# Moving the tiles of a two-layer hybrid block to other SBUF addresses

## The chip, the cores and the metric

The kernel runs on one NeuronCore of a Trainium2 chip. The metric is the device time of one execution in microseconds (us). The kernel before was timed three times: 1871.41, 1870.98 and 1871.26 us, a median of 1871.26 us. A profiled execution of it took 1871.55 us, and the trace's span, from the first instruction to the last, is 1869.8 us of that.

## The reference

The reference computes two layers of a hybrid block on 512 tokens of width 1024, in float32. Cut to what matters:

```python
def hybrid_layer(x, ...):
    h = rms_norm(x, g_pre_mix)
    proj = h @ w_in                                  # 1024 -> 6728 columns
    q, k, v, qi, ki, wi, xr, gr, zu, zv, gate_logits = split(proj)
    q, k, qi, ki = partial rope of each
    y_a = dsa_attention(q, k, v, qi, ki, wi)         # top 128 keys by an indexer, softmax, values
    y_b = rg_lru(causal_depthwise_conv(xr)) * gelu(gr)
    y_c = chunked_spatial_gating(gelu(zu), rms_norm(gelu(zv)), w_spatial, b_spatial)
    branch = einsum('nbsw,nwd->nbsd', stack([y_a, y_b, y_c]), w_branch)
    merged = einsum('bsnd,nbsd->bsd', sigmoid(gate_logits), branch)
    x = x + rms_norm(merged @ w_out, g_post_mix)
    f = square(relu(rms_norm(x, g_pre_ffn) @ w_ffn_up)) @ w_ffn_down
    x = x + rms_norm(f, g_post_ffn)
    ple = (p_i @ w_ple) * sigmoid(x @ w_ple_gate)
    return x + rms_norm(ple, g_post_ple)
```

## The kernel before

**Products in three passes.** Activations are held transposed: 8 tiles of 128 features by 512 tokens. Each float32 operand is split into a high part that fits the matmul's fp32r type and a low rest, and each product is made of three matmuls into one PSUM bank: high weights with high activations, low weights with high activations, high weights with low activations. That is `mm3` (lines 289 to 292), called by `gemm` once for each 128 rows of the contraction:

```python
def mm3(ps, wh, wl, xh, xl, start, stop):
    PE.matmul(ps, wh, xh, start=start, stop=False)     # L290
    PE.matmul(ps, wl, xh, start=False, stop=False)     # L291
    PE.matmul(ps, wh, xl, start=False, stop=stop)      # L292
```

The second argument is the stationary operand (128 x 128, loaded anew for each matmul, PEld in the profile) and the third is the moving operand, 512 columns wide in most calls and 256 in some. `gemm_arriving` (matmuls on L348) does the same for four outputs at a time while its input tiles are still being made. `tokens` (L585) swaps the roles: slices of the activations are stationary and the weights move.

**Weights.** 303 weight tiles of 128 x 1024 float32 come from HBM on SP's queue into a rotation of three buffers `wr`. ScalarE (ACT) casts each into `wh` (L235) and VectorE (DVE) makes the rest `wl` (L236); `wh` and `wl` have four buffers each. `getw` starts the preparation three tiles ahead.

**Activations.** `xh0` to `xl7` hold the split input of a gemm. Slots `A0` to `A7`, `B0` to `B7` (512 columns each), `K0`, `K1`, `V0`, `V1` (4 x 512 columns each) and `M0` to `M7` are used again and again: for queries and keys, for the branches' outputs, for the merged value, and for the hidden layer of the feed-forward part. `tmp` is a rotation of 11 tiles of 128 x 512 for everything short-lived. `sacc` sums squares for the norms, which GpSimd (POOL) adds up on L390.

**Order.** Every engine runs its own queue in the order in which the program issues its instructions, and waits on semaphores where a tile is read or is to be written again. The side work (index scores, top 128, attention, recurrence) is issued in pieces between the matmuls by a small planner, `tick` and `run_tasks`, with due times written in the code.

**Where a tile lies.** Three pools hold the SBUF tiles: `cp` (persistent tiles, slots and small vectors), `wp` (`wr`, `wh`, `wl`) and `tp` (`tmp`). The pools follow each other in one column of addresses, the same in all 128 partitions. Within a pool, tiles lie in the order in which they are first asked for, each padded to 32 bytes. So a small vector asked for between two large tiles shifts all that follows. A tile of 128 bytes that nothing uses, `lead`, stands ahead of `xh0`. A 512-column float32 tile takes 2048 bytes of a partition. The remainder of a tile's address after division by 2048 is called its offset from here on.

Of the kernel before, what the change touches and what calls it, by code (L numbers as in the profile page):

```python
# [8 lines left out]
F32 = mybir.dt.float32  # L9
F32R = mybir.dt.float32r  # L10
BF16 = mybir.dt.bfloat16
I32 = mybir.dt.int32
# [5 lines left out]
S = 512  # L18
D = 1024
KT = 8  # L20
# [22 lines left out]
NVEC = 76  # L43


def f32v(ap):
    return ap.bitcast(F32)
# [3 lines left out]
def hybrid_block_kernel(ctx, tc, xT, pT, pos, vec, bsp, freq, w_in, w_tok, w_lru, w_sp, w_br, w_out, w_up, w_dn, w_ple, w_gate, out, depth=DEPTH, dbg=None):  # L51
# [3 lines left out]
    cp = ctx.enter_context(tc.tile_pool(name="cp", bufs=1))  # L55
    wp = ctx.enter_context(tc.tile_pool(name="wp", bufs=1))
    tp = ctx.enter_context(tc.tile_pool(name="tp", bufs=1))
    pp = ctx.enter_context(tc.tile_pool(name="pp", bufs=1, space=PSUM))

    uid = [0]  # L60

    def nm(p):
        uid[0] += 1
        return f"{p}_{uid[0]}"

    def tmp(dt=F32):
        return tp.tile([128, S], dt, tag="tmp", name=nm("tmp"), bufs=NTMP)

    def small(n, tag="sm", bufs=8):
        return cp.tile([128, n], F32, tag=tag, name=nm(tag), bufs=bufs)  # L70

    def bank():
        return pp.tile([128, 512], F32, tag="ps", name=nm("ps"), bufs=8)

    def slot(tag, dt=F32, big=False):
        return cp.tile([128, 4, S] if big else [128, S], dt, tag=tag, name=nm(tag))
# [8 lines left out]
    NWB = 4  # L85
    LAG = 1
    TAIL = 3
    ATT = 13
    WARM = 120
    FIRST = [0, 1, 4]  # L90


    X = [cp.tile([128, S], F32, tag=f"X{k}", name=f"X{k}") for k in range(KT)]
    ident = cp.tile([128, 128], F32, tag="ident", name="ident")
    make_identity(nc, ident)
    warm = cp.tile([128, 1], F32, tag="warm", name="warm")
    V.memset(warm, 0.0)
    A.activation(warm, warm, AF.Square)
    ones2 = cp.tile([128, 2], F32, tag="ones2", name="ones2")
    V.memset(ones2, 1.0)  # L100
    mhalf = cp.tile([128, 4], F32, tag="mhalf", name="mhalf")
    V.memset(mhalf, -0.5)
    BIAS = [cp.tile([128, 128 * (t + 1)], BF16, tag=f"bias{t}", name=f"bias{t}") for t in range(4)]

    V.memset(BIAS[3], 1.0)
    wps = bank()
    for _ in range(WARM):
        PE.matmul(wps[:, 0:64], BIAS[3][:, 0:128], BIAS[3][:, 0:64], start=True, stop=True)


    tri = BIAS[0]
    G.memset(tri, 0.0)
    G.affine_select(out=tri, in_=tri, compare_op=ALU.is_ge, fill=NEG, base=0, pattern=[[-1, 128]], channel_multiplier=1)
    fq = cp.tile([128, 8], F32, tag="fq", name="fq")
    posi = cp.tile([128, 4], I32, tag="posi", name="posi")

    ropeC = cp.tile([128, S], F32, tag="ropeC", name="ropeC")
    ropeS = cp.tile([128, S], F32, tag="ropeS", name="ropeS")

# [104 lines left out]
    def prep():  # L224
        i = nprep[0]
        nprep[0] += 1
        key, src = order[i]
        raw = wp.tile([128, 1024], F32, tag="wr", name=nm("wr"), bufs=3)
        nc.sync.dma_start(raw, src)
        if key[0] == "sp":  # L230
            r3 = raw.rearrange("p (g t) -> p g t", g=8)
            G.affine_select(out=r3, in_=r3, compare_op=ALU.is_ge, fill=0.0, base=0, pattern=[[0, 8], [1, 128]], channel_multiplier=-1)
        hi = wp.tile([128, 1024], F32R, tag="wh", name=nm("wh"), bufs=NWB)
        lo = wp.tile([128, 1024], F32R, tag="wl", name=nm("wl"), bufs=NWB)
        A.copy(hi, raw)  # L235
        V.tensor_sub(lo, raw, f32v(hi))  # L236
        prepared[key] = (hi, lo)
# [15 lines left out]
    def defer(us, fn):  # L253
        later.append((clk[0] + us, uid[0], fn))
        uid[0] += 1
# [8 lines left out]
    def add_task(q, gen):  # L264
        q["wait"].append(gen)
# [17 lines left out]
    def finish(q):  # L283
        run_later(force=True)
        while q["act"] or q["wait"]:
            tick(0.3)
# [39 lines left out]

    def gemm_arriving(keys, xs, source, ranges, arrived=None, lag=LAG, tail=TAIL):


        n = len(keys)  # L330
        ws = [getw(key, 0) for key in keys[:-1]]
        pss = [bank() for _ in keys]
        last = {}
        for r in ranges:
            gen = source(r)
            for k in range(KT):
                with ordered(last):
                    next(gen)
                    todo = [(o, k) for o in range(len(ws))]
                    if len(ws) < n and k == lag:  # L340
                        ws.append(getw(keys[-1], 0))
                        todo += [(n - 1, q) for q in range(k + 1)]
                    if r is ranges[-1] and k >= KT - tail:
                        todo = [] if k < KT - 1 else [(o, q) for o in range(n) for q in range(KT - tail, KT)]
                    for i, (o, q) in enumerate(todo):
                        h3, l3 = [v.rearrange("p (k c) -> p k c", k=KT) for v in ws[o]]
                        for m in range(3):
                            PE.matmul(pss[o][:, r], (h3, l3, h3)[m][:, q], xs[q][m // 2][:, r], start=q == 0 and m == 0, stop=q == KT - 1 and m == 2)  # L348
                        if r is ranges[-1] and q == KT - 1 and o < n - 1:
                            prep()  # L350
                tick(0.65 * len(todo) * width(r) / S)
            if arrived is not None:
                arrived(r)
        while nprep[0] < nget[0] + LA:
            prep()
        return pss
# [103 lines left out]
                tick(0.1)  # L460
            return self.gens[r.start]


    cp.tile([128, 32], F32, tag="lead", name="lead")
    XS = [(slot(f"xh{k}", F32R), slot(f"xl{k}", F32R)) for k in range(KT)]

    def x_tiles(r, xs, g=None, st=None, ys=None, bc=None, gp=None, on_g=()):
# [3 lines left out]
        def updated(d):  # L471
            if ys is not None and d < KT:
                if gp is None:
                    V.tensor_mul(ys[d][:, r], ys[d][:, r], bc)
                else:
                    V.scalar_tensor_tensor(ys[d][:, r], ys[d][:, r], gp[:, d:d + 1], bc, op0=ALU.mult, op1=ALU.mult)
                (G if d in on_g else V).tensor_add(X[d][:, r], X[d][:, r], ys[d][:, r])  # L477

        updated(0)
        for d in range(KT):  # L480
            x = X[d][:, r]
            if xs is not None:
# [14 lines left out]
                    V.scalar_tensor_tensor(lo, x, g[:, d:d + 1], f32v(hi), op0=ALU.mult, op1=ALU.subtract)  # L497
            yield d

    vecs = [cp.tile([128, NVEC], F32, tag=f"vec{l}", name=f"vec{l}") for l in range(depth)]  # L500
    nc.sync.dma_start(vecs[0], vec[0])
    nc.scalar.dma_start(posi, pos)
    nc.scalar.dma_start(fq, freq)

    chunks = []
    for key, src in order[:3]:
        raw = wp.tile([128, 1024], F32, tag="wr", name=nm("wr"), bufs=3)
        hi = wp.tile([128, 1024], F32R, tag="wh", name=nm("wh"), bufs=NWB)
        lo = wp.tile([128, 1024], F32R, tag="wl", name=nm("wl"), bufs=NWB)
        prepared[key] = (hi, lo)  # L510
        chunks.append((src, raw, hi, lo))
    nprep[0] = 3
    for k in range(KT):
        if k in FIRST:
            c = slice(128 * k, 128 * (FIRST + [KT])[FIRST.index(k) + 1])
            for src, raw, hi, lo in chunks:
                nc.sync.dma_start(raw[:, c], src[:, c])
        nc.sync.dma_start(X[k], xT[k])

# [8 lines left out]
    for l in range(depth):  # L528
# [19 lines left out]
        rt = st.rt  # L548
        first = gemm_arriving([("in", l, f"xr{j}") for j in range(3)], XS, norm.source if l else lambda r: gen0, HALVES if l else (FULL,), st.row(D, R), 0, TAIL if l else 1)

        def proj(name, ahead=LA):
            ps = bank()
            gemm(ps, getw(("in", l, name), ahead), XS, KT)
            return ps
# [11 lines left out]
        def rope(ps, n=128):  # L566
            t1, u = tmp(), tmp()
            V.tensor_mul(t1[:n], ps[:n], Cr[:n])
            V.stream_shuffle(u[:n], ps[:n], mask=SHUF)
            G.tensor_mul(u[:n], u[:n], Sr[:n])  # L570
            G.tensor_add(t1[:n], t1[:n], u[:n])  # L571
            return t1
# [108 lines left out]
        def select(t, sc):  # L681
# [20 lines left out]
            G.tensor_add(gt[:, :n], gt[:, :n], eq[:, :n])  # L702
            G.tensor_scalar(BIAS[t], gt[:, :n], -NEG, NEG, op0=ALU.mult, op1=ALU.add)
            yield 1.0
# [47 lines left out]
        for j in range(4):  # L752
            mx = tmp()
# [49 lines left out]
        sp8 = small(4, "sp8", 2)  # L803
        V.tensor_scalar(sp8, h, 8.0, None, op0=ALU.mult)
        nsp8 = small(4, "nsp8", 2)
# [86 lines left out]
        def attention(j):  # L892
# [6 lines left out]
            def logits(t):  # L899
                n = 128 * (t + 1)  # L900
                pr = qk(q2, kk, (ql, ql), kk, slice(t * 128, (t + 1) * 128), max(n, 256))
                for s in range(2):
# [5 lines left out]

                    V.tensor_tensor_reduce(lt, pr[s][:, :n], BIAS[t], scale=-ATT_SCALE, scalar=3.0e38, op0=ALU.add, op1=ALU.min, accum_out=mx[:, 0:1])
                    A.activation(lt, lt, AF.Exp, scale=-1.0, bias=mx[:, 0:1], accum_out=mx[:, 1:2])  # L910
# [82 lines left out]
        for j in range(4):  # L993
            f = rope(proj(f"q{j}"))
# [8 lines left out]
            if j == 0:  # L1003
                finish(idxq)
            defer(ATT, lambda j=j: add_task(attq, attention(j)))
            gated(1, YB, ds=range(2 * j, 2 * j + 2))
# [113 lines left out]
        gp = small(8, "gp", 2)  # L1120
# [12 lines left out]
    for r in HALVES:  # L1133
        for d in norm.source(r):
            (nc.sync if d % 2 == 0 else nc.scalar).dma_start(out[d, :, r], X[d][:, r])

# [76 lines left out]
```

## Time and profile before

| | before |
|---|---|
| median of three runs | 1871.26 us (1870.98 to 1871.41) |
| the profiled execution | 1871.55 us |
| its span in the trace | 1869.8 us |
| PE busy | 1825.9 us (98%), 8798 matmuls |
| PEld busy (weight loads) | 1503.1 us (80%), 8798 loads |
| DVE, ACT, POOL busy | 1158.4, 802.4, 365.8 us (62, 43, 20%) |
| DMA | 167.77 MB, mean 90 GB/s; the weights' queue 27% of the 16 engines' span |
| TensorE clock | 0.992 of full speed on average |

PE is TensorE's matmuls, PEld its weight loads, which run beside them. Matmuls overlap in the trace: one that "takes" 391 ns is followed by the next after some 230 ns. So the pace of TensorE is read from the distance between starts, not from the mean duration.

### The profile page before, as it was taken

The page shows a single profiled execution, that of the slowest core. Times are in us where ns is not written, and L with a number is a line of the kernel's source. Part 1 is how long each engine was busy: PE and PEld are TensorE (multiplying, and loading weights), DVE is VectorE, ACT ScalarE, POOL GpSimd, SP SyncE. Part 2 cuts the span into 40 slices and gives each one's busy share as a digit, 9 for nine tenths or more (in the row PEclk, how much of TensorE's full clock was granted, in tenths as well). Part 3 has the DMA queues.
Part 4 walks back from the last instruction along what each step waited for, and adds up shares of the span by engine and source line. Part 5 has one row for each costly group of instructions (what it writes and reads, how often), then busy time and mean ns, then how long its engine had stood idle before and what let it go on. Part 6 is the DMA issues. An engine that isn't in the chain of part 4 may idle for free.

```text
span 1869.8 us, 22869 instructions
## 1 busy us (share of the span) xinstructions
PE 1825.9 (98%) x8798; PEld 1503.1 (80%) x8798; DVE 1158.4 (62%) x1939; ACT 802.4 (43%) x1292; POOL 365.8 (20%) x292
## 2 busy tenths in 40 slices
PE   8999999999999999999999999999999999999997
PEld 7678777788888888888886787887888888888886
DVE  6689976666286253533686999666563852535355
ACT  5466436564453222223444572455544432222233
POOL 3513222210240000003454141222003200000033
PEclk9999999999999999999999999999999999999998
DMA  5122222222223322332212222222222223232321
GB/s 171 62 91 84 97 91 91 68 80 79 86 84 104 100 93 99 95 109 90 91 58 95 69 90 99 94 80 69 90 79 91 91 90 102 92 100 92 111 79 57
DMA packets 49679, 167.77 MB, mean 90 GB/s; under 512 B 6049, under 2 KB 8865, under 8 KB 49569
## 3 DMA queue, kind: packets, MB, share of 16 engines
q1 hardware_dynamic: 47376, 163.64, 27.0%
q10 hardware_dynamic: 2192, 2.67, 0.5%
q8 instruction: 69, 1.13, 0.3%
q14 instruction: 42, 0.34, 0.1%
HBM read 164.19 MB, written 2.10 MB: 89 GB/s over the span
## 4 chain that ended last, share of the span: by engine, by line
PE 74%; DVE 11%; POOL 6%; issue 5%; ACT 4%; DMA 0%; SPq 0%; POOLq 0%; ACTq 0%; DVEq 0%
PE ps L290 21%; PE ps L292 20%; PE ps L291 20%; PE ps L348 4%; PE ps L585 4%; DVE tmp L689 2%; DVE wl L236 2%; DVE m L687 2%; POOL tmp L570 1%; POOL tmp L571 1%; PE ps L937 1%; PE ps L654 1%; PE ps L651 1%; POOL sacc L390 1%; POOL X L477 1%
## 5 line engine op out<-in xcount | busy, mean ns | idle before, releaser
L235 ACT CAST wh<-wr 128x1024 fp32r<-128x1024 f32 x303 | 317.0, 1049 | 468.7 <-PE ps L292 382.8
L236 DVE TENSOR_TENSOR wl<-wr,wh 128x1024 fp32r<-128x1024 f32 x303 | 386.2, 1278 | 201.8 <-ACT wh L235 201.7
L290 PE MATMUL ps<-xh,wh 128*128 128x512 f32 (+1 forms) x1296 | 506.9, 391 | 0.0
L292 PE MATMUL ps<-xl,wh 128*128 128x512 f32 (+1 forms) x1296 | 498.1, 384 | 0.0
L291 PE MATMUL ps<-xh,wl 128*128 128x512 f32 (+1 forms) x1296 | 495.7, 382 | 0.8 <-DVE wl L236 0.8
L390 POOL TENSOR_TENSOR sacc<-sacc,tmp 128x256 f32<-128x256 f32 (+1 forms) x99 | 110.3, 1115 | 902.9 <-issue 590.1
L292 PEld LDWEIGHTS ps<-xl,wh 128*128 128x128 f32 x1296 | 243.4, 188 | 50.1
L290 PEld LDWEIGHTS ps<-xh,wh 128*128 128x128 f32 x1296 | 243.7, 188 | 49.4 <-issue 4.9
L291 PEld LDWEIGHTS ps<-xh,wl 128*128 128x128 f32 x1296 | 243.7, 188 | 46.9 <-DVE wl L236 1.7
L292 PE MATMUL ps<-V,wh 128*128 128x512 f32 (+1 forms) x528 | 196.8, 373 | 0.0
L290 PE MATMUL ps<-K,wh 128*128 128x512 f32 (+1 forms) x432 | 159.9, 370 | 0.0
L291 PE MATMUL ps<-K,wl 128*128 128x512 f32 (+1 forms) x432 | 157.9, 366 | 0.0
L292 PE MATMUL ps<-B,wh 128*128 128x512 f32 x336 | 131.9, 392 | 0.0
L290 PE MATMUL ps<-A,wh 128*128 128x512 f32 x320 | 126.6, 396 | 0.0
L291 PE MATMUL ps<-A,wl 128*128 128x512 f32 x320 | 124.8, 390 | 0.0
L1072 DVE TENSOR_TENSOR M<-M,ps 128x512 f32<-128x512 f32 x48 | 33.1, 689 | 143.8 <-PE ps L292 143.8
L292 PEld LDWEIGHTS ps<-V,wh 128*128 128x128 f32 x528 | 99.3, 188 | 18.5
L1060 DVE TENSOR_TENSOR tmp<-ps,R 128x512 f32<-128x512 f32 x64 | 43.8, 689 | 111.5 <-PE ps L292 111.5
L348 PE MATMUL ps<-xl,wh 128*128 128x256 f32 (+1 forms) x264 | 88.4, 335 | 7.8 <-DVE xl L497 7.2
L291 PEld LDWEIGHTS ps<-K,wl 128*128 128x128 f32 x432 | 81.2, 188 | 14.3
L290 PEld LDWEIGHTS ps<-K,wh 128*128 128x128 f32 x432 | 81.3, 188 | 13.2
L348 PE MATMUL ps<-xh,wh 128*128 128x256 f32 (+1 forms) x264 | 87.1, 330 | 0.5 <-ACT xh L487 0.5
(239 smaller groups left out, 2745.5 us busy)
## 6 DMA issues: line engine op xcount, KB each, us to landing
wr<-in_w_in_dram SPq DMA_DIRECT2D x95, 512.0 KB, 3.3
wr<-in_w_up_dram SPq DMA_DIRECT2D x64, 512.0 KB, 3.3
wr<-in_w_dn_dram SPq DMA_DIRECT2D x64, 512.0 KB, 3.3
wr<-in_w_br_dram SPq DMA_DIRECT2D x24, 512.0 KB, 3.3
wr<-in_w_tok_dram SPq DMA_DIRECT2D x16, 512.0 KB, 3.3
wr<-in_w_out_dram SPq DMA_DIRECT2D x16, 512.0 KB, 3.3
wr<-in_w_gate_dram SPq DMA_DIRECT2D x16, 512.0 KB, 3.3
X<-in_xT_dram SPq DMA_DIRECT2D x8, 256.0 KB, 5.8
```

The costliest lines, as they stand in the source:

```text
L235: A.copy(hi, raw)
L236: V.tensor_sub(lo, raw, f32v(hi))
L290: PE.matmul(ps, wh, xh, start=start, stop=False)
L291: PE.matmul(ps, wl, xh, start=False, stop=False)
L292: PE.matmul(ps, wh, xl, start=False, stop=stop)
L348: PE.matmul(pss[o][:, r], (h3, l3, h3)[m][:, q], xs[q][m // 2][:, r], start=q == 0 and m == 0, stop=q == KT - 1 and m == 2)
L390: G.tensor_add(sacc[:, r], sacc[:, r], self.q[r.start, r.stop])
L585: PE.matmul(ps, x, w, start=k == 0 and i == 0, stop=k == KT - 1 and i == 2)
L687: V.max(m8, (sc if r == 0 else wk)[:, :n])
L689: V.match_replace(wk[:, :n], m8, (sc if r == 0 else wk)[:, :n], -3.0e38)
L1060: V.tensor_mul(t, ps, R)
L1072: V.tensor_add(F[d], F[d], ps)
```

## The change

No instruction is added, removed or moved. On every engine the order of instructions and what each waits for are the same as before, but for one name: the tile that a first ACT instruction warms up with is now one of the `sm` vectors. Only the addresses of the tiles differ:

- All small vectors (`sm`, `rt`, `wi`, `m8`, `cnt`, `sp8`, `nsp8`, `mx`, `gp`, `vec0`) are asked for first and lie at the head of `cp`. The constants and masks (`ident`, `ones2`, `mhalf`, the bias tiles, `fq`, `posi`, `vec1`) go to a new pool `ep`, behind `tmp`.
- An unused tile of 256 bytes fills `cp` up so that `X0` begins at 18432, which is 9 x 2048. What follows in `cp`, and `wr` behind it, comes in tiles of 2048, 4096 or 8192 bytes.
- Behind `wr` an unused tile of 128 bytes shifts `wh`, `wl` and `tmp`.

The offsets, address modulo 2048 bytes, before and after:

| tiles | before | after |
|---|---|---|
| `X0` to `X7` | 128 | 0 |
| `ropeC`, `ropeS`, `sacc` | 1312 | 0 |
| `xh`, `xl` | 1440 | 0 |
| `R` | 160 | 0 |
| `B0` to `B7`, `M0`, `M1`, `M4` to `M7` | 416 | 0 |
| `A0` to `A7`, `K0`, `K1`, `V0`, `V1` | 672 | 0 |
| `M2`, `M3` | 928, 1056 | 0 |
| `wr` | 1376 | 0 |
| `wh`, `wl`, `tmp` | 1376 | 128 |

A weight tile of 4096 bytes is read in slices of 128 columns, 512 bytes apart, so a stationary slice lies at 1376 plus a multiple of 512 before and at 128 plus a multiple of 512 after.

```diff
@@ pools
     tp = ctx.enter_context(tc.tile_pool(name="tp", bufs=1))
+    ep = ctx.enter_context(tc.tile_pool(name="ep", bufs=1))
@@ head of the kernel
+    LEAD = 256
+    GAP = 32
...
-    X = [cp.tile([128, S], F32, tag=f"X{k}", name=f"X{k}") for k in range(KT)]
-    ident = cp.tile([128, 128], F32, tag="ident", name="ident")
+    for n, tag, bufs in ((4, "sm", 8), (4, "rt", 4), (32, "wi", 2), (8, "m8", 4), (1, "cnt", 4), (4, "sp8", 2), (4, "nsp8", 2), (2, "mx", 8), (8, "gp", 2)):
+        small(n, tag, bufs)
+    vecs = [(ep if l else cp).tile([128, NVEC], F32, tag=f"vec{l}", name=f"vec{l}") for l in range(depth)]
+    gap = [False]
+
+    def wraw():
+        raw = wp.tile([128, 1024], F32, tag="wr", name=nm("wr"), bufs=3)
+        if not gap[0]:
+            gap[0] = True
+            wp.tile([128, GAP], F32, tag="gap", name="gap")
+        return raw
+    ident = ep.tile([128, 128], F32, tag="ident", name="ident")
...
-    BIAS = [cp.tile([128, 128 * (t + 1)], BF16, tag=f"bias{t}", name=f"bias{t}") for t in range(4)]
+    BIAS = [ep.tile([128, 128 * (t + 1)], BF16, tag=f"bias{t}", name=f"bias{t}") for t in range(4)]
...
+    cp.tile([128, LEAD // 4], F32, tag="lead", name="lead")
+    X = [cp.tile([128, S], F32, tag=f"X{k}", name=f"X{k}") for k in range(KT)]
     ropeC = cp.tile([128, S], F32, tag="ropeC", name="ropeC")
...
@@ prep, and the first three weight tiles
-        raw = wp.tile([128, 1024], F32, tag="wr", name=nm("wr"), bufs=3)
+        raw = wraw()
@@ ahead of xh0
-    cp.tile([128, 32], F32, tag="lead", name="lead")
     XS = [(slot(f"xh{k}", F32R), slot(f"xl{k}", F32R)) for k in range(KT)]
```

## Rows read from the trace of the kernel before

**Rows 1.** The page: engines' busy time, share of the span, instructions.

```profile
PE 1825.9 (98%) x8798; PEld 1503.1 (80%) x8798; DVE 1158.4 (62%) x1939; ACT 802.4 (43%) x1292; POOL 365.8 (20%) x292
```

**Rows 2.** The page: the chain that ended last, by engine.

```profile
PE 74%; DVE 11%; POOL 6%; issue 5%; ACT 4%; DMA 0%; SPq 0%; POOLq 0%; ACTq 0%; DVEq 0%
```

**Rows 3.** Timeline of PE, a feed-forward gemm: start, us, engine, line, tiles.

```profile
630.27 0.39 PE L290 MATMUL ps<-K,wh 128*128 128x512 f32 x1
...
652.24 0.40 PE L290 MATMUL ps<-K,wh 128*128 128x512 f32 x1
```

**Rows 4.** The same view, a feed-forward gemm on `A` and `B`.

```profile
700.31 0.39 PE L290 MATMUL ps<-A,wh 128*128 128x512 f32 x1
...
722.28 0.39 PE L290 MATMUL ps<-A,wh 128*128 128x512 f32 x1
```

**Rows 5.** The chain in order of time: start, us, engine, line, count.

```profile
886.24 21.97 PE ps L348 x96
```

**Rows 6.** Timeline of PE, the output projection, the same tiles as in the feed-forward gemm.

```profile
471.96 0.40 PE L290 MATMUL ps<-K,wh 128*128 128x512 f32 x1
...
494.36 0.40 PE L290 MATMUL ps<-K,wh 128*128 128x512 f32 x1
```

**Rows 7.** Timeline of PE, `tokens`: weights move, activations are stationary.

```profile
233.04 0.39 PE L585 MATMUL ps<-wh,xh 128*128 128x512 f32 x1
...
237.24 0.39 PE L585 MATMUL ps<-wh,xh 128*128 128x512 f32 x1
```

**Rows 8.** Timeline of PE, `tokens` in a stretch at the lower clock.

```profile
1003.89 0.63 PE L585 MATMUL ps<-wl,xh 128*128 128x512 f32 x1
...
1006.03 0.63 PE L585 MATMUL ps<-wh,xl 128*128 128x512 f32 x1
```

**Rows 9.** Busy time by stretch, PE alone: that stretch, with its granted clock.

```profile
1003.90:1006.40 2.50, 2.50 (x7) 0.50 0.85 252
```

**Rows 10.** Timeline of PE, spatial gating, 256 columns, weights move.

```profile
130.28 0.28 PE L290 MATMUL ps<-wh,K 128*128 128x256 f32 x1
...
130.63 0.28 PE L290 MATMUL ps<-wh,K 128*128 128x256 f32 x1
...
130.98 0.28 PE L290 MATMUL ps<-wh,K 128*128 128x256 f32 x1
...
132.91 0.28 PE L292 MATMUL ps<-wl,K 128*128 128x256 f32 x1
```

**Rows 11.** Timeline of PE, a gemm in halves, 256 columns.

```profile
1839.73 0.28 PE L290 MATMUL ps<-xh,wh 128*128 128x256 f32 x1
...
1840.91 0.28 PE L291 MATMUL ps<-xh,wl 128*128 128x256 f32 x1
```

**Rows 12.** Groups by line and shape, PE: count, busy us, mean ns, idle before.

```profile
L290 PE MATMUL ps<-xh,wh 128*128 128x512 f32 x1200 | 479.8, 400 | 0.0
...
L585 PE MATMUL ps<-wh,xh 128*128 128x512 f32 x128 | 53.2, 415 | 0.0
...
L292 PE MATMUL ps<-A,wh 128*128 128x512 f32 x64 | 25.4, 397 | 0.0
```

**Rows 13.** The same view, 256 columns.

```profile
L348 PE MATMUL ps<-xl,wh 128*128 128x256 f32 x176 | 52.4, 298 | 4.0 <-DVE xl L497 3.5
...
L292 PE MATMUL ps<-V,wh 128*128 128x256 f32 x96 | 26.8, 279 | 0.0
```

**Rows 14.** The same view, DVE, 512 columns.

```profile
L1061 DVE SCALAR_TENSOR_TENSOR tmp<-tmp 128x512 f32<-128x512 f32 x64 | 43.8, 689 | 1.6
L1060 DVE TENSOR_TENSOR tmp<-ps,R 128x512 f32<-128x512 f32 x64 | 43.8, 689 | 111.5 <-PE ps L292 111.5
...
L362 DVE TENSOR_TENSOR B<-tmp,A 128x512 fp32r<-128x512 f32 x32 | 21.9, 684 | 0.0
...
L362 DVE TENSOR_TENSOR V<-tmp,K 128x512 fp32r<-128x512 f32 x32 | 21.5, 683 | 1.4 <-ACT K L361 1.4
```

**Rows 15.** The page: DMA queues, then the weights' issues with time to landing.

```profile
q1 hardware_dynamic: 47376, 163.64, 27.0%
...
wr<-in_w_in_dram SPq DMA_DIRECT2D x95, 512.0 KB, 3.3
```

More of the change, by code (lines that the diff above doesn't have):

```diff
@@ L90, in hybrid_block_kernel @@
     FIRST = [0, 1, 4]
-    X = [cp.tile([128, S], F32, tag=f"X{k}", name=f"X{k}") for k in range(KT)]
-    ident = cp.tile([128, 128], F32, tag="ident", name="ident")
+    for n, tag, bufs in ((4, "sm", 8), (4, "rt", 4), (32, "wi", 2), (8, "m8", 4), (1, "cnt", 4), (4, "sp8", 2), (4, "nsp8", 2), (2, "mx", 8), (8, "gp", 2)):
[9 more added lines that the diff above has]
+    ident = ep.tile([128, 128], F32, tag="ident", name="ident")
     make_identity(nc, ident)
-    warm = cp.tile([128, 1], F32, tag="warm", name="warm")
+    warm = small(1)
     V.memset(warm, 0.0)
     A.activation(warm, warm, AF.Square)
-    ones2 = cp.tile([128, 2], F32, tag="ones2", name="ones2")
+    ones2 = ep.tile([128, 2], F32, tag="ones2", name="ones2")
     V.memset(ones2, 1.0)
-    mhalf = cp.tile([128, 4], F32, tag="mhalf", name="mhalf")
+    mhalf = ep.tile([128, 4], F32, tag="mhalf", name="mhalf")
     V.memset(mhalf, -0.5)
-    BIAS = [cp.tile([128, 128 * (t + 1)], BF16, tag=f"bias{t}", name=f"bias{t}") for t in range(4)]
+    BIAS = [ep.tile([128, 128 * (t + 1)], BF16, tag=f"bias{t}", name=f"bias{t}") for t in range(4)]
     V.memset(BIAS[3], 1.0)
@@ L113, in hybrid_block_kernel @@
     G.affine_select(out=tri, in_=tri, compare_op=ALU.is_ge, fill=NEG, base=0, pattern=[[-1, 128]], channel_multiplier=1)
-    fq = cp.tile([128, 8], F32, tag="fq", name="fq")
-    posi = cp.tile([128, 4], I32, tag="posi", name="posi")
+    fq = ep.tile([128, 8], F32, tag="fq", name="fq")
+    posi = ep.tile([128, 4], I32, tag="posi", name="posi")
+    cp.tile([128, LEAD // 4], F32, tag="lead", name="lead")
+    X = [cp.tile([128, S], F32, tag=f"X{k}", name=f"X{k}") for k in range(KT)]
     ropeC = cp.tile([128, S], F32, tag="ropeC", name="ropeC")
@@ L498, in x_tiles @@
             yield d
-    vecs = [cp.tile([128, NVEC], F32, tag=f"vec{l}", name=f"vec{l}") for l in range(depth)]
     nc.sync.dma_start(vecs[0], vec[0])
@@ L506, in hybrid_block_kernel @@
     for key, src in order[:3]:
-        raw = wp.tile([128, 1024], F32, tag="wr", name=nm("wr"), bufs=3)
+        raw = wraw()
         hi = wp.tile([128, 1024], F32R, tag="wh", name=nm("wh"), bufs=NWB)
```

## The prediction

> **What bounds the kernel now.** The page comes first. TensorE is busy 98% of the span [rows 1], and the chain that ended last runs through it for 74% and through four other parts for the rest, none over 11% [rows 2]. DMA has 0% of that chain; the weights' queue fills 27% of the DMA engines' time and a tile lands 3.3 us after its issue [rows 2, 15]. So the pace of TensorE decides, and since the change moves no instruction, only a different duration or pace can change the time.
>
> That pace is read from starts in the timeline of the engine. In a feed-forward gemm 96 matmuls of 512 columns start between 630.27 and 652.24 us: 21.97 / 96 = 228.9 ns each [rows 3]. A gemm on other slots gives the same 21.97 us for 96 [rows 4], and so does a stretch on `xh` and `xl` [rows 5]. At 2.4 GHz 512 columns take 213.3 ns, so 15.6 ns of each interval are extra.
>
> Three places show that this extra isn't fixed. The output projection runs through the same tiles K, V, `wh` and `wl`, and takes 22.40 us for 96: 233.3 ns, an extra of 20.0 [rows 6]. `tokens`, where weights move and activations stand, has 18 intervals in 4.20 us, 233.3 ns again [rows 7]. In a stretch at a granted clock of 0.50, which is the level of 1.2 GHz, five intervals of `tokens` take 2.14 us, 428 ns each, where 512 columns at that clock need 426.7 [rows 8, 9]: the extra is gone. It is a cost that shows only while the array asks for its data at the full clock. The spatial gating shows how it can go away without any change in clock: its first three intervals of 256 columns take 0.35 us (117 ns), the next three again 0.35, and then 17 take 1.93 us, 113.5 ns each, to the end of the stretch [rows 10]. A common gemm in halves has ten intervals in 1.18 us, 118 ns [rows 11]. I read this as two streams of reads, the moving operand of one matmul and the stationary operand of the next, that get in each other's way until a slip puts them apart. That reading is mine; no row names the streams.
>
> **What the change does to each part.** All activation slots had an address of 160 modulo 256 bytes before, and the weights 96. So every gemm in the trace has one and the same distance between its two operands modulo 256, which is 64, and each operand is 32 past a multiple of 64. The equal pace of rows 3 to 5 says only that distances that differ by multiples of 256 are alike. After the change the distance is 128 modulo 256, and every tile lies on a multiple of 128. No row shows such a pair. That is the unknown cost.
>
> Elementwise work: nothing. DVE's operations on 512 columns take 683 to 689 ns whether both tiles have one offset (`tmp` to `tmp`), two, or one of them is in PSUM [rows 14]. A tile at a new offset should take the same. The transfers hold the same bytes and hide behind 73% of idle DMA time; if that cover failed, the first sign would be the casts of ACT on L235 waiting for a DMA.
>
> TensorE: bounds from both sides. The most that can go is the extra itself, 228.9 - 213.3 - 1.3 = 14.3 ns a matmul of 512 columns, with the 1.3 that the lower clock leaves. The most that any row shows it to grow by is 233.3 - 228.9 = 4.4 ns. Between them, as a gain, lies the distance from the halves' 118 ns [rows 11] to the 113.5 that the spatial gating reaches [rows 10], 4.5 ns a matmul; I take it, because the gating is the one place where the same instructions with the same tiles are seen to lose part of the extra and to stay without it. The sum:
>
> - L290 to L292 and L348 have 6360 matmuls of 512 columns in 17 groups, from x1200 to x64 [rows 12], and 1104 of 256 columns in nine groups, from x176 to x96 [rows 13]. 7464 x 4.5 ns = 33.6 us.
> - `tokens` has 384 matmuls (three groups of x128 [rows 12]). From 233.3 to 228.9 - 4.5 = 224.4 it would gain 8.9 ns each, 3.4 us.
> - The output projection's five full-width gemms, 120 matmuls a layer, lose their slower pace: 240 x 4.4 ns = 1.1 us.
>
> Together 38.1 us. Not all of it reaches the end: where TensorE waits for a norm, an exponent or the index scores, it would only wait longer. The share that counts lies between the chain's 74% [rows 2] and the 98% of busy time [rows 1]; the middle, 86%, gives 32.8 us. Against the profiled execution's own 1871.55 us, which is 0.3 over the median, that is 1839 us. With the gain between a tenth and twice this size the case runs from 1806 to 1868.
>
> One rule of the Trainium skill speaks against any gain. By "SBUF — State Buffer", section "Who interferes with whom", TensorE has two read ports of its own, one for the moving operand and one for the weight load, and never waits on another engine. By it the pace can't depend on where tiles lie and the time stays at 1871. The equal pace of rows 3 to 5 agrees with it, the unequal pace of rows 3 and 6 on the same tiles neither agrees nor disagrees, and the step within rows 10 speaks against a pace fixed by the instruction alone.
>
> **Rivals.**
>
> *The addresses don't matter.* Then the extra comes from how loads and matmuls are handed on, and 233.3 against 228.9 on the same tiles is a state into which the engine falls after a stall. For it: rows 3 to 5 are equal to a hundredth of a microsecond at three offsets, and rows 3 and 6 differ with equal addresses. Against it: nothing in the trace has a different distance modulo 256, so it was not tried. Time: 1871.
>
> *The slower pace becomes the rule.* The mechanism is the same meeting of reads, at every gemm of 512 columns, with the new distance the worse one. `tokens`, where the operands' roles and so the sign of the distance are swapped, never left 233.3 ns in its steady stretches; the new distance of 128 modulo 256 is the same in both directions, so the gemms would stand with `tokens`. Price: 4.4 ns for each of 6360 - 240 = 6120 matmuls, 26.9 us, and by the same 4.4 ns on 1104 of 256 columns 4.9 us more, all paid, since a later TensorE delays everything: up to 1903, and 1898 for the wide ones alone. It decides as soon as more matmuls go to 233.3 than leave it, which is any net growth of the extra over 0.6 ns a matmul. Against it: spatial gating has the swapped sign as well, and it got faster.
>
> *The whole extra goes.* With all tiles on multiples of 128 each matmul keeps only the 1.3 ns of rows 8. 6360 x 14.3 = 90.9 us, 1104 x (118 - 106.7 - 1.3) = 11.0, `tokens` 384 x 18.7 = 7.2, the projection 1.1: 110 us, of which 86% is 95 us: 1777. The Trainium skill's "TensorE: Matmul & The Clock Gate", section "Wait — 56ns, not 53.3ns?", gives a warm interval of columns over 2.4 GHz plus about 2.5 ns, for bf16 operands; by it the wide matmuls would come to 215.8 ns. No interval in this trace of a wide matmul at the full clock comes near it in a steady stretch, and what else separates fp32r from it isn't shown, so the chance is small.
>
> **How the numbers follow.** A gain of part of the extra: 0.50. The whole extra: 0.06. No change: 0.16. The slower pace: 0.28, near 1898 where all gemms take it and between 1876 and 1898 where some do. About 0.2% of the time, 3.7 us, is what can be told from no change here. So faster 0.56, same 0.16, slower 0.28. The forecast is 1839 us. Its own range is 1806 to 1868. Since slower holds more than a quarter, the range for 8 in 10 goes up to 1900, which takes in 1898 and leaves out what halves would add, and down to 1800, which leaves out the whole extra's 1777.
>
> **What would show it.** Right: in the timeline, 96 intervals on K and V in about 21.5 us instead of 21.97, the same for the output projection instead of 22.40, `tokens` at the common pace, halves at 113 to 114 ns, and DVE's groups unchanged at 683 to 689 ns. Wrong in the pace: intervals of 228.9 as before (the first rival) or 233.3 in the feed-forward part (the second). Wrong elsewhere: DVE, ACT or POOL durations that moved by more than 1%, or L235 waiting for a DMA. The forecast falls with the reading of rows 10: if that step was not a matter of where and when operands are read, a new distance has no reason to bring it about.

## The result and the profile after

The time rose. The median of four runs is 1883.65 us (1882.89 to 1886.62) against 1871.34 us (1870.98 to 1872.86) of before in the same comparison: a ratio of 1.0065, 95% interval 1.0051 to 1.0079. The forecast was 1839 us; the time lies within the range, on the rival's side. The profiled execution of after was the slowest of its four (1886.62 us, span 1884.9), so the two traces differ by 15.1 us where the medians differ by 12.3.

The page of after, busy time by engine and then the chain that ended last:

```profile
PE 1844.0 (98%) x8798; PEld 1506.2 (80%) x8798; DVE 1158.3 (61%) x1939; ACT 802.6 (43%) x1292; POOL 366.1 (19%) x292
...
PE 78%; DVE 8%; POOL 6%; ACT 4%; issue 4%; DMA 0%; SPq 0%; POOLq 0%; ACTq 0%; DVEq 0%
```

Against [rows 1, 2] PE grew by 18.1 us and its weight loads by 3.1; DVE, ACT and POOL moved by 0.3 us at most. DVE's share of the chain fell from 11% to 8%; what the waits themselves lost is read below. (L290 to L292 are now L306 to L308, L348 is L364, L585 is L598.)

Groups of DVE on 512 columns, by line and shape, answer to [rows 14] within 1 ns:

```profile
L1074 DVE SCALAR_TENSOR_TENSOR tmp<-tmp 128x512 f32<-128x512 f32 x64 | 43.8, 690 | 1.6
L1073 DVE TENSOR_TENSOR tmp<-ps,R 128x512 f32<-128x512 f32 x64 | 43.8, 689 | 116.0 <-PE ps L308 116.0
...
L378 DVE TENSOR_TENSOR V<-tmp,K 128x512 fp32r<-128x512 f32 x32 | 21.5, 683 | 1.4 <-ACT K L377 1.4
```

So the pace of TensorE is what is left. The timeline of PE of after, start and us first: the first and last start of 96 intervals of the feed-forward gemm of [rows 3], then the same for the output projection of [rows 6], 18 intervals of `tokens` [rows 7], and 23 of the spatial gating [rows 10].

```profile
632.62 0.40 PE L306 MATMUL ps<-K,wh 128*128 128x512 f32 x1
...
654.93 0.39 PE L306 MATMUL ps<-K,wh 128*128 128x512 f32 x1
...
472.98 0.40 PE L306 MATMUL ps<-K,wh 128*128 128x512 f32 x1
...
495.38 0.40 PE L306 MATMUL ps<-K,wh 128*128 128x512 f32 x1
...
232.72 0.39 PE L598 MATMUL ps<-wh,xh 128*128 128x512 f32 x1
...
236.89 0.39 PE L598 MATMUL ps<-wh,xh 128*128 128x512 f32 x1
...
130.77 0.28 PE L306 MATMUL ps<-wh,K 128*128 128x256 f32 x1
...
133.50 0.28 PE L308 MATMUL ps<-wl,K 128*128 128x256 f32 x1
```

The feed-forward gemm takes 22.31 us for 96: 232.4 ns each, 3.5 more than before. The output projection keeps its 22.40 us, 233.3 ns, in layer 1 (in layer 2 it comes to 232.3). This stretch of `tokens` comes to 4.17 / 18 = 231.7 ns, 1.6 less; the others lie between 232.4 and 233.3, near the pace of before. The gating runs at a mean of 2.73 / 23 = 118.7 ns; the step down to 113.5 that it made before is gone. The chain in order of time shows the stretch of [rows 5], once in each layer, at 233.3 and at 232.4 ns:

```profile
893.11 22.40 PE ps L364 x96
...
1825.12 22.31 PE ps L364 x96
```

Where the 15.1 us went, from the first matmul to the last, with the same matmul in both traces as the bound of each stage. The columns on the right split the change: what the intervals of 512 columns grew by in sum (those between 215 and 250 ns in both traces), the same for 256 columns (108 to 130 ns), and the rest, which is waits above all.

| stage | before, us | after, us | change | 512 columns | 256 columns | rest |
|---|---|---|---|---|---|---|
| start | 31.45 | 30.38 | -1.1 | +0.1 | 0 | -1.2 |
| mixer, layer 1 | 507.07 | 509.89 | +2.8 | +3.7 | +0.7 | -1.6 |
| feed-forward and gate, layer 1 | 367.94 | 373.49 | +5.55 | +5.6 | 0 | 0 |
| mixer, layer 2 | 558.01 | 560.10 | +2.1 | +3.5 | +1.3 | -2.7 |
| feed-forward and gate, layer 2 | 368.01 | 373.45 | +5.44 | +5.5 | 0 | 0 |
| end | 27.13 | 27.41 | +0.3 | +0.1 | +0.3 | -0.1 |

In the feed-forward stages nothing is won back and TensorE pays the slower pace in full: 11.0 of 15.1 us. In the mixers 9.2 us of slower matmuls come down to 4.9, because the rest shrinks by 4.3. The waits of PE of after (engine, line waited for: us, times, longest) show one that shrank:

```profile
PE ps L364 <- DVE xl L511: 5.7, 9, 2.4
```

Before, the same nine waits took 7.2 us in all, the longest 3.8. Not all shrank: the eight waits for `A`, made on L651 (L638 before), went from 7.1 to 8.2 us.

### The profile page after: what moved, and what is told of

Its sections match the earlier page's. It is cut to its first block, busy times and chain, and to the rows that moved or that the text cites. A ratio compares the mean times of both kernels' runs of the same rounds, so it can differ in the third digit from the quotient of the medians.

```text
span 1884.9 us, 22869 instructions
## 1 busy us (share of the span) xinstructions
PE 1844.0 (98%) x8798; PEld 1506.2 (80%) x8798; DVE 1158.3 (61%) x1939; ACT 802.6 (43%) x1292; POOL 366.1 (19%) x292
## 4 chain that ended last, share of the span: by engine, by line
PE 78%; DVE 8%; POOL 6%; ACT 4%; issue 4%; DMA 0%; SPq 0%; POOLq 0%; ACTq 0%; DVEq 0%
PE ps L306 22%; PE ps L308 22%; PE ps L307 22%; PE ps L598 4%; PE ps L364 3%; POOL tmp L583 1%; POOL tmp L584 1%; PE ps L950 1%; PE ps L667 1%; POOL sacc L406 1%; DVE tmp L702 1%; DVE wl L252 1%; PE ps L664 1%; POOL X L491 1%; DVE m L700 1%
## 5 line engine op out<-in xcount | busy, mean ns | idle before, releaser
L306 PE MATMUL ps<-xh,wh 128*128 128x512 f32 (+1 forms) x1296 | 509.6, 393 | 0.0
L308 PE MATMUL ps<-xl,wh 128*128 128x512 f32 (+1 forms) x1296 | 500.5, 386 | 0.0
L306 PEld LDWEIGHTS ps<-xh,wh 128*128 128x128 f32 x1296 | 244.1, 188 | 54.0 <-issue 4.9
L308 PEld LDWEIGHTS ps<-xl,wh 128*128 128x128 f32 x1296 | 244.0, 188 | 52.8
L308 PE MATMUL ps<-V,wh 128*128 128x512 f32 (+1 forms) x528 | 197.7, 374 | 0.0
L306 PE MATMUL ps<-K,wh 128*128 128x512 f32 (+1 forms) x432 | 160.0, 370 | 0.0
L308 PE MATMUL ps<-B,wh 128*128 128x512 f32 x336 | 132.6, 395 | 0.0
L306 PE MATMUL ps<-A,wh 128*128 128x512 f32 x320 | 126.6, 395 | 0.0
L308 PEld LDWEIGHTS ps<-V,wh 128*128 128x128 f32 x528 | 99.5, 188 | 18.8
L364 PE MATMUL ps<-xl,wh 128*128 128x256 f32 (+1 forms) x264 | 88.0, 333 | 6.4 <-DVE xl L511 5.7
L306 PEld LDWEIGHTS ps<-K,wh 128*128 128x128 f32 x432 | 81.4, 188 | 15.0
L364 PE MATMUL ps<-xh,wh 128*128 128x256 f32 (+1 forms) x264 | 86.7, 328 | 2.8 <-ACT xh L501 2.8
```

## The experiments

The theory, D in the expectations: the pace of a steady gemm depends on the distance between the stationary tile and the moving one, modulo 256 bytes. I count it with its sign, stationary minus moving; for a gemm that is `wh`, `wl` minus the activation slots. Before has 96 - 160, which is 192 modulo 256, and after has 128. Its rivals: the start of a tile within 64 bytes (all tiles on multiples of 128 or not), the order of the tiles and their lying at multiples of 2048, `tmp` (which moved with the weights), and W, the writes of ACT and DVE into the weight tiles. All kernels compute the whole reference. Each was timed in three rounds beside before; [..] is the 95% interval of the ratio.

**e1_no_gap**: after without the 128 bytes, distance 0.

```diff
-            wp.tile([128, GAP], F32, tag="gap", name="gap")
```

> The changed kernel without the 128 unused bytes ahead of wh: all large tiles at offset 0, weights and activations 0 apart. Theory D (the distance between the moving and the stationary operand, modulo 256, sets TensorE's pace): a distance that no run has shown, so a pace other than 232.4 ns per 512-column matmul, most likely worse, 233.3 or more, 1888 us or more. Rival A (what counts is where a tile starts within 64 bytes, 0 against 32 before): 232.4 ns, 1884 us as with the gap. Rival O (something else of the new order of tiles): 1884 us.

Measured: 1861.19 us, ratio 0.9949 [0.9934, 0.9964], faster than both. The timeline of PE, 96 intervals of the feed-forward gemm and then of the output projection:

```profile
619.69 0.39 PE L306 MATMUL ps<-K,wh 128*128 128x512 f32 x1
...
641.45 0.39 PE L306 MATMUL ps<-K,wh 128*128 128x512 f32 x1
...
472.89 0.39 PE L306 MATMUL ps<-K,wh 128*128 128x512 f32 x1
...
494.65 0.39 PE L306 MATMUL ps<-K,wh 128*128 128x512 f32 x1
```

Both take 21.76 us: 226.7 ns. The output projection, at 233.3 before and after, has no slower pace of its own here. The gap of 128 bytes is what costs. D had left the pace open and guessed a slower one; that guess missed.

**e2_shift32**: every tile 32 bytes further, the distance still 128.

```diff
-    LEAD = 256
+    LEAD = 288
```

> The changed kernel with everything from X0 on 32 bytes further: activations at 32, weights at 160, the distance of 128 kept. Theory D: 232.4 ns, 1884 us. Rival A: back to 228.9 ns per matmul and about 1871 us. Rival O: 1884 us.

Measured: 1885.52 us, 1.0074 [1.0059, 1.009], and the same 22.31 us for 96 as after:

```profile
619.76 0.40 PE L306 MATMUL ps<-K,wh 128*128 128x512 f32 x1
...
642.07 0.39 PE L306 MATMUL ps<-K,wh 128*128 128x512 f32 x1
```

A common shift of both operands by 32 bytes changes nothing.

**e3_gap192**: the distance of before, with the tiles in after's order.

```diff
-    GAP = 32
+    GAP = 48
```

> The changed kernel with 192 unused bytes ahead of wh: activations at 0, weights at 192, which is the distance of before modulo 256. Theory D: 228.9 ns, 1871 us. Rival A: 232.4 ns, 1884 us. Rival O: 1884 us.

Measured: 1871.5 us, 0.9995 [0.9986, 1.0005], and before's pace:

```profile
619.65 0.39 PE L306 MATMUL ps<-K,wh 128*128 128x512 f32 x1
...
641.63 0.39 PE L306 MATMUL ps<-K,wh 128*128 128x512 f32 x1
```

21.98 us for 96, 229.0 ns [rows 3]. 64 bytes more undo the whole loss; the new order and the multiples of 2048 are worth nothing by themselves.

**e4_offsets_of_before**: in addition the remainders modulo 256 of before, 160 and 96.

```diff
-    LEAD = 256
-    GAP = 32
+    LEAD = 416
+    GAP = 48
```

> The changed kernel with activations at 160 and weights at 96 modulo 256, the offsets of before, but in the new order of tiles. Theory D and rival A both: 228.9 ns, 1871 us. Rival O: 1884 us.

Measured: 1871.68 us, 0.9999 [0.999, 1.0009], again 21.98 us for 96. As e3: the difference counts, not the remainders.

The traces of e4 and e3 also show that the distance alone doesn't fix the pace. The timeline of PE of e4, 96 intervals of the output projection in layer 1 and in layer 2, the same gemm on the same tiles at the same addresses:

```profile
473.80 0.39 PE L306 MATMUL ps<-K,wh 128*128 128x512 f32 x1
...
495.77 0.39 PE L306 MATMUL ps<-K,wh 128*128 128x512 f32 x1
...
1398.17 0.40 PE L306 MATMUL ps<-K,wh 128*128 128x512 f32 x1
...
1420.57 0.40 PE L306 MATMUL ps<-K,wh 128*128 128x512 f32 x1
```

Layer 1 takes 21.97 us, 228.9 ns a matmul, and layer 2 takes 22.40, 233.3. In e3 it is the other way round. Layer 1 takes 22.40 us there, and layer 2:

```profile
1397.90 0.39 PE L306 MATMUL ps<-K,wh 128*128 128x512 f32 x1
...
1419.87 0.39 PE L306 MATMUL ps<-K,wh 128*128 128x512 f32 x1
```

That is 21.97 us. So at 192 a stretch of wide matmuls runs at either of two paces, and the 233.3 ns of [rows 6] are not a property of the output projection.

**e5_before_plus64**: the kernel before with 64 unused bytes between `wr` and `wh`, distance 0.

```diff
         raw = wp.tile([128, 1024], F32, tag="wr", name=nm("wr"), bufs=3)
+        if not chunks:
+            wp.tile([128, 16], F32, tag="gap", name="gap")
```

> The kernel before with one edit: 64 unused bytes between wr and wh, so that wh, wl and tmp are a multiple of 256 from all activation slots, which stay at 160 modulo 256 and at three different offsets modulo 2048. Theory D (the distance modulo 256 alone): 226.7 ns per 512-column matmul and 1861 us, as with no gap in the changed kernel. Rival E (both at multiples of 2048 is what made that run faster): 228.9 ns, 1871 us.

Measured: 1861.74 us, 0.9947 [0.9932, 0.9962]:

```profile
619.94 0.39 PE L290 MATMUL ps<-K,wh 128*128 128x512 f32 x1
...
641.70 0.39 PE L290 MATMUL ps<-K,wh 128*128 128x512 f32 x1
```

226.7 ns as in e1. The old layout, with small vectors between the large tiles, gains as much from a distance of 0 as the new one. The gap also moves `wh` against `wr`: that distance is 0 in before and 192 in e3, 0 in e1 and 64 here, at equal times, so it isn't what counts.

**e6_gap64, e7_gap32, e8_gap224, e11_gap96, e12_gap160**: the other multiples of 32.

```diff
-    GAP = 32
+    GAP = 16    # e6; e7: 8, e8: 56, e11: 24, e12: 40
```

> The changed kernel with 64 unused bytes ahead of wh: weights 64 past the activations. By theory D this is the distance that tokens had before, where activations stood and weights moved: the gemms at 233.3 ns, tokens at 228.9, and about 1887 us (3.5 ns more gave 12.3 us, so 4.4 give 15). Rival S (only the size of the distance counts, 64 either way): 228.9 ns and 1871 us.

> The changed kernel with 32 unused bytes ahead of wh: a distance that no run has shown. Theory D, with a pace that grows from 226.7 ns at 0 to 233.3 at 64: between them, about 230 ns and 1875 us. Rival N (only the line of 64 bytes in which an operand starts counts): 226.7 ns and 1861 us as at 0, or 233.3 as at 64.

> The changed kernel with 224 unused bytes ahead of wh: weights 32 short of a multiple of 256 past the activations. Theory D, between 192 (228.9 ns, 1871 us) and 0 (226.7 ns, 1861 us): 227.8 ns, 1866 us, unless the least lies on this side of 0, then under 226.7 ns and under 1861 us. Rival N: 228.9 or 226.7.

> The changed kernel with 96 unused bytes ahead of wh. Known so far: 226.7 ns at a distance of 0, 233.3 at 32 and 64, 232.4 at 128, 228.9 at 192, 233.3 at 224. Theory D with odd multiples of 32 as the worst: 233.3 ns, 1888 us. Rival M (a smooth curve between 64 and 128): 232.9 ns, 1886 us.

> The changed kernel with 160 unused bytes ahead of wh. Theory D with odd multiples of 32 as the worst: 233.3 ns, 1888 us. Rival M (a smooth curve between 128 and 192): 230.6 ns, 1877 us.

All distances, each pace from 96 intervals of the feed-forward gemm:

| distance | kernel | ns a matmul | median, us | ratio to before |
|---|---|---|---|---|
| 0 | e1 | 226.7 | 1861.19 | 0.9949 [0.9934, 0.9964] |
| 32 | e7 | 233.3 | 1889.96 | 1.0094 [1.0077, 1.0111] |
| 64 | e6 | 233.3 | 1888.02 | 1.0089 [1.0074, 1.0104] |
| 96 | e11 | 234.3 | 1893.72 | 1.0117 [1.0102, 1.0132] |
| 128 | after | 232.4 | 1883.65 | 1.0065 [1.0051, 1.0079] |
| 160 | e12 | 233.3 | 1890.94 | 1.0102 [1.0087, 1.0117] |
| 192 | e3 | 229.0 | 1871.5 | 0.9995 [0.9986, 1.0005] |
| 224 | e8 | 233.3 | 1888.92 | 1.0094 [1.0079, 1.0109] |

0 and 192 stand out; the other six lie within 2 ns. D foresaw that the distance matters, but not each new pace: e6 and e12 came as expected, but e7 (expected at about 230 ns) and e8 (227.8) came to 233.3, and e11 went beyond both D's 233.3 and rival M's 232.9. What D amounts to is this table. The rivals fail one by one: A on e2 and e3, O on e3, E on e5, S on e6, N on e8, M on e12.

e6 also tests the sign: by D its `tokens`, where weights move, has 192 and must come to the pace that gemms had before. The timeline of PE of e6: the feed-forward gemm (96 intervals), `tokens` (12), a gemm in halves (48), and the spatial gating, where weights move (23):

```profile
620.17 0.40 PE L306 MATMUL ps<-K,wh 128*128 128x512 f32 x1
...
642.57 0.40 PE L306 MATMUL ps<-K,wh 128*128 128x512 f32 x1
...
234.76 0.39 PE L598 MATMUL ps<-wh,xh 128*128 128x512 f32 x1
...
237.51 0.39 PE L598 MATMUL ps<-wh,xh 128*128 128x512 f32 x1
...
502.63 0.28 PE L306 MATMUL ps<-K,wh 128*128 128x256 f32 x1
...
508.07 0.28 PE L306 MATMUL ps<-K,wh 128*128 128x256 f32 x1
...
131.34 0.28 PE L306 MATMUL ps<-wh,K 128*128 128x256 f32 x1
...
134.05 0.28 PE L308 MATMUL ps<-wl,K 128*128 128x256 f32 x1
```

Gemm 233.3, `tokens` 2.75 / 12 = 229.2: the two have swapped places against [rows 3, 7], as D says.

For 256 columns these lines, halves at 5.44 / 48 = 113.3 ns and gating at 2.71 / 23 = 117.8, look like the same swap against [rows 10, 11], but other stretches show that it is none. The timeline of PE of e6 again, 48 intervals of halves on `xh`, at the same distance of 64, and then of e3, distance 192, 48 intervals of one gemm in halves in layer 1 and in layer 2:

```profile
923.50 0.28 PE L306 MATMUL ps<-xh,wh 128*128 128x256 f32 x1
...
929.15 0.28 PE L306 MATMUL ps<-xh,wh 128*128 128x256 f32 x1
...
502.01 0.28 PE L306 MATMUL ps<-K,wh 128*128 128x256 f32 x1
...
507.67 0.28 PE L306 MATMUL ps<-K,wh 128*128 128x256 f32 x1
...
1425.00 0.28 PE L306 MATMUL ps<-K,wh 128*128 128x256 f32 x1
...
1430.44 0.28 PE L306 MATMUL ps<-K,wh 128*128 128x256 f32 x1
```

They take 5.65, 5.66 and 5.44 us: 117.7, 117.9 and 113.3 ns. So at 64 and at 192 alike a stretch of 256 columns runs at about 117.8 or at 113.3, with the same tiles. At none of the six other distances do twelve successive intervals average less than 116.2.

**e9_tmp_alone**: the weights at distance 0, the 128 bytes behind `wl`, so that `tmp` alone lies 128 past.

```diff
@@ wraw
-            wp.tile([128, GAP], F32, tag="gap", name="gap")
@@ the first weight tiles, behind wl
+        if not chunks:
+            wp.tile([128, GAP], F32, tag="gap", name="gap")
```

> The kernel without the gap (weights and activations at 0), but with 128 unused bytes between wl and tmp, so that tmp alone lies 128 past. Theory D: what counts are the two operands of the gemms, so 226.7 ns and 1861 us. Rival T (tmp's distance from what DVE, ACT and GpSimd read beside it costs time): part of the 23 us that lie between the runs with and without the gap, 1866 us or more at an unchanged 226.7 ns.

Measured: 1860.17 us, 0.9937 [0.992, 0.9954], 21.76 us for 96, so rival T fails: the place of `tmp` costs nothing.

**e10_wl_alone**: `wl` alone 128 past; `wh` and `tmp` at distance 0.

```diff
@@ wraw
-            wp.tile([128, GAP], F32, tag="gap", name="gap")
@@ the first weight tiles, between wh and wl
+        if not chunks:
+            wp.tile([128, GAP], F32, tag="gap", name="gap")
@@ behind wl
+        if not chunks:
+            wp.tile([128, GAP], F32, tag="gap2", name="gap2")
```

> The kernel without the gap, but with wl alone 128 past; wh and tmp at 0. Theory D with the load of the next matmul's weights as the one that meets the moving operand: only the interval that begins with L306's matmul, beside which wl is loaded, keeps the extra of the distance 128; the three intervals differ, their mean is (232.4 + 2 x 226.7) / 3 = 228.6 ns, 1867 us. Theory D with the matmul's own weights: the same mean, the long interval begins with L307's matmul. Rival W (the writing of wh and wl by ACT and DVE is what meets the matmuls' reads): no fixed order of long and short intervals.

Measured: 1879.84 us, 1.0045 [1.003, 1.006], 231.1 ns on average. D's size missed: one matmul in three with `wl` was to bring 228.6 ns and 1867 us. The timeline of PE of e10, successive starts:

```profile
640.13 0.40 PE L306 MATMUL ps<-K,wh 128*128 128x512 f32 x1
640.36 0.40 PE L307 MATMUL ps<-K,wl 128*128 128x512 f32 x1
640.60 0.39 PE L308 MATMUL ps<-V,wh 128*128 128x512 f32 x1
640.82 0.40 PE L306 MATMUL ps<-K,wh 128*128 128x512 f32 x1
```

The gaps between starts are 0.23, 0.24, 0.22 us, over many triples 232.5, 234.2 and 226.7 ns, always in this order. Two intervals of each three are slow: the one that begins with the matmul ahead of `wl`, beside which `wl` is loaded, and the one that begins with `wl`'s own. Only from L308 to the next L306, with no `wl` in either, does distance 0 show. So a shifted tile costs in two intervals, not one. The order fixed to the line also speaks against W: writes of ACT and DVE don't come in step with each third matmul.

## Why the prediction was wrong

**The bound.** Right: the pace of TensorE decided, and it was read in the right place. Elementwise work and transfers at nothing: right, the groups of [rows 14] moved by 1 ns at most, and DMA stays at 0% of the chain.

**The unknown.** Right that the new pair of addresses is the one open cost and that no row shows that pair. Wrong in "every gemm in the trace has one and the same distance between its two operands modulo 256". Without the sign it is 64 everywhere; with it, gemms have 192, and `tokens` and the gating have 64. So the trace did hold two distances, and at 512 columns it showed them: 228.9 ns at 192 [rows 3 to 5], 233.3 at 64 [rows 7]. "Nothing in the trace has a different distance modulo 256" is wrong too: the attention's products on L651 pair `K` with `A`, 0 apart, but only two at a time, which gives no steady pace.

**The step that failed** is the choice of 4.5 ns as a gain, "because the gating is the one place where the same instructions with the same tiles are seen to lose part of the extra and to stay without it". The step in [rows 10] is real: the gating makes it after five intervals in all its stretches in the traces of before, e3 and e4. But it leads to one of two paces that 256 columns have at the distances 64 and 192. Wide matmuls have two paces as far apart at 192, 233.3 and 228.9, and the feed-forward gemms of before ran at the faster one already [rows 3, 6]. So I priced a gain that they had behind them, at a new distance for which nothing spoke for it: at 128 no twelve successive intervals of 256 columns average less than 117.8 ns, and the gating stays at 118.7. In place of -4.5 ns the wide matmul's term measured +3.5 (228.9 to 232.4 in the feed-forward gemms).

**The bounds.** "The most that any row shows it to grow by", 4.4 ns, held for the change; e11's 5.4 lies above it. The 14.3 ns that could go at most were never approached: the best of eight distances gave 2.2. The slower pace in before also covers more than the projection's 240 matmuls: the gemm on `A` ahead of it too, some 390 in both layers.

**The share that counts.** 86% was too much. In the traces 20.8 us of steady growth (18.5 of it at 512 columns) became 15.1 at the end, 73%. Between the fastest and the slowest kernel, e9 (226.7 ns, 1860.17 us) and e11 (234.3, 1893.72), one nanosecond is worth 33.55 / 7.6 = 4.4 us, where 6360 wide matmuls would make 6.4, or 69%.

**The rivals.** "The slower pace becomes the rule" was the case, in so far as the new distance is the worse one for the wide gemms, and with its remark that gemms would stand with `tokens` at 128: 232.4 and 231.7 to 233.3. That two reads meet is not shown. Its price was too high: 3.5 instead of 4.4 ns, and not "all paid". "The addresses don't matter" falls with e1, e3 and e5, but its second half holds: 233.3 against 228.9 on the same tiles is a state of the stretch (e3, e4). That a stall brings it on is not shown. The Trainium skill's "SBUF — State Buffer", section "Who interferes with whom", gives TensorE two independent read ports, for the moving operand and for the weight load, and lets it wait on nobody. That section of the Trainium skill says nothing of addresses; the prediction took from it that the pace can't depend on them. These runs don't agree: the distance of the two operands moves it from 226.7 to 234.3 ns, and the measurement decides.

**Open.** No row names what the two reads meet in, so why 0 and 192 are good is not shown. What sends a stretch into the one or the other of two paces at one distance isn't either, nor whether the same stretches take it in each execution, since each kernel has one trace; at 0 the question goes away for 512 columns, with 226.7 to 227.3 ns over each 96. Distances that aren't multiples of 32 were not tried, nor other shapes than 256 and 512 columns.

## What to carry to other kernels

Where TensorE never waits and still stays above its columns' time, read the distance between starts and compare the addresses of its two operands, with the sign: here 64 bytes of padding in one place took 0.5% off (e5), and the change with its 128 put 0.65% on. Put stationary and moving tiles at one remainder modulo 256 first, then time the neighbours, and read each width by itself: 256 columns gained nothing at 0. Read a pace from several stretches before giving it a cause: one stretch at each distance would have shown a swap at 256 columns that isn't there. A step seen at one shape and one pair of addresses is no price for another until an experiment moves that pair alone.

## What the runs showed of the hardware

- The pace of fp32r matmuls of 512 columns changes with addresses alone, in the feed-forward gemms: 226.7 ns at distance 0, 229.0 at 192, 232.4 to 234.3 elsewhere. The sign counts: 64 and 192 are 4.3 ns apart.
- One distance can have two paces, each steady over a stretch: 228.9 and 233.3 ns for 512 columns at 192 (e3, e4), 113.3 and 117.8 for 256 columns at 64 and at 192 (e3, e6).
- 0 is no gain for 256 columns: 120.0 ns in the gating (e1: 20 intervals in 2.40 us), against 118.7 at 128.
- A shifted stationary tile slows two intervals, the one beside which it is loaded and the one that begins with its own matmul (e10).
- At 128 single intervals go from 228 to 241 ns in a pattern that repeats each seven matmuls (feed-forward gemm of after); the sum of seven stays at 1626 to 1627 ns, so only long stretches can be compared.
